# A channel shuffle in 28 tiles in place of 24: most tiles 20 KB a partition instead of 24 KB, five load buffers instead of four

## The chip, the cores and the metric

The kernel runs on 1 core of one Trainium2 chip. The metric is the device time of one execution in microseconds (us). The experiments ran in three batches on three chips, each batch with its own runs of the kernel before, so differences are taken within a batch.

## The reference

The input is 16 x 64 x 64 x 256 float32 (67.1 MB). In each row of 256 channels, 8 groups of 32 channels are transposed to 32 groups of 8. Nothing is computed.

```python
x = x.reshape(batch, h, w, groups, channels_per_group)
x = x.transpose(0, 1, 2, 4, 3)
x = x.reshape(batch, h, w, c)
```

## The kernel before

The array is cut into tiles of 128 partitions. A size `q` of the list below is in rows of 256 floats, so in KB, a partition. Each tile is loaded by one transfer from the SP queue, copied with the shuffle by the Vector engine (DVE), and stored by one transfer from the ACT queue. All buffers of a pool are as large as the largest tile.

```python
_SIZES = [4, 4, 8] + [24] * 20 + [16]
_IN_BUFS = 4
_OUT_BUFS = 4
...
    first = 0
    for q in _SIZES:
        in_tile = in_pool.tile([P, biggest * c], F32, name="in_tile")
        nc.sync.dma_start(out=in_tile[:, : q * c], in_=rows(x_flat, first, q))
        out_tile = out_pool.tile([P, biggest * c], F32, name="out_tile")
        nc.vector.tensor_copy(
            out=out_tile[:, : q * c].rearrange("p (i j g) -> p i j g", j=CPG, g=G),
            in_=in_tile[:, : q * c].rearrange("p (i g j) -> p i j g", g=G, j=CPG),
        )
        nc.scalar.dma_start(out=rows(out_flat, first, q), in_=out_tile[:, : q * c])
        first += P * q
...
```

Of the kernel before, what the change touches and what calls it, by code (L numbers as in the profile page):

```python
# [1 line left out]

# [4 lines left out]


F32 = mybir.dt.float32
P = 128  # L10

_SIZES = [4, 4, 8] + [24] * 20 + [16]
_IN_BUFS = 4
_OUT_BUFS = 4


@with_exitstack
def kernel(
    ctx: ExitStack,
    tc: tile.TileContext,  # L20
    x: bass.AP,
    groups: bass.AP,
    out: bass.AP,
):
    nc = tc.nc
    b, h, w, c = x.shape
    G = int(groups)
    CPG = c // G
    assert G * CPG == c
    assert sum(_SIZES) * P == b * h * w  # L30
    biggest = max(_SIZES)

    x_flat = x.rearrange("b h w c -> (b h w c)")
    out_flat = out.rearrange("b h w c -> (b h w c)")

    in_pool = ctx.enter_context(tc.tile_pool(name="in_pool", bufs=_IN_BUFS))
    out_pool = ctx.enter_context(tc.tile_pool(name="out_pool", bufs=_OUT_BUFS))

    def rows(flat, first, q):

        return flat[first * c : (first + P * q) * c].rearrange("(p f) -> p f", p=P)

    ctx.enter_context(tc.manual_schedule(engines=None))
# [13 lines that stand above are left out]
# [1 line left out]
_INS = ['x', 'groups']  # L58
_OUTS = [((16, 64, 64, 256), 'float32')]

_NUMBERS = {'groups': 8}


# [26 lines left out]
```

## Time and profile before

| kernel before | |
|---|---|
| time | 317.67 us, median of 3 (317.63 to 317.87) |
| profiled span | 315.2 us |
| DVE busy | 122.2 us, 39% |
| two DMA queues together | 99.4% of 16 engines |
| bytes | 134.22 MB, half in, half out |

How to read it: the two DMA shares are of the span of all 16 engines, so their sum says how much bandwidth is left. The lines themselves are in the prediction. Two more views matter later, and the prediction does not show them. The first is the order of instructions around one load's issue. In the order of instructions the columns are start, length (us), engine, line, operation; an SPq row is a load being issued, an ACTq row a store.

```profile
107.54 5.69 DVE L49 COPY out_tile<-in_tile 128x6144 f32<-128x6144 f32 x1 [8.81 <-DMA in_tile<-in_x_dram]
113.26 0.33 SPq L47 DMA_DIRECT2D in_tile<-in_x_dram  x1
113.27 0.36 ACTq L53 DMA_DIRECT2D out_dram<-out_tile  x1
```

The copy ends at 113.23 us, and only then is the next load issued, into the buffer that the copy has emptied. The second is the other half of the load queue's waits. The prediction quotes only its waits for copies (98.0 us); the same answer has a larger line above it, in which the queue waits for an earlier load to land:

```profile
SPq L47 <- DMA in_tile<-in_x_dram: 124.7, 17, 8.4
```

In each turn the queue first waited for that landing and then, 5.8 us more, for the copy.

### The profile page before, as it was taken

What the parts mean: (1) busy time and instruction counts of PE and PEld (TensorE: products, weight loads), DVE (VectorE), ACT (ScalarE), POOL (GpSimd) and SP (SyncE); (2) the same over time, 40 slices, a digit from 0 to 9 for tenths busy, and PEclk for the clock granted to TensorE, in tenths of its full rate; (3) what the DMA queues carried; (4) which work ended last, traced back from release to release, by engine and by line L of the source; (5) the groups of instructions that cost most, each with busy time, mean ns of one, the idle gap of its engine ahead of it and who ended that gap; (6) DMA issues with size and microseconds to landing.
All of it is one profiled execution on the core that took longest, in us unless ns stands there. A gap on an engine that the chain in (4) does not pass through costs nothing.

```text
span 315.2 us, 178 instructions
## 1 busy us (share of the span) xinstructions
DVE 122.2 (39%) x24; POOL 0.2 (0%) x4
## 2 busy tenths in 40 slices
DVE  2277517070625335260707162442517070625400
POOL 0000000000000000000000000000000000000000
DMA  8999999999999999999999999999999999999997
GB/s 316 399 458 407 423 424 446 430 421 446 437 415 446 437 418 443 440 415 443 440 415 443 443 412 443 446 409 443 446 415 437 446 415 437 443 420 431 431 437 319
DMA packets 6912, 134.22 MB, mean 426 GB/s; under 512 B 768, under 2 KB 768, under 8 KB 1280
## 3 DMA queue, kind: packets, MB, share of 16 engines
q1 hardware_dynamic: 3456, 67.11, 49.9%
q10 hardware_dynamic: 3456, 67.11, 49.5%
HBM read 67.11 MB, written 67.11 MB: 426 GB/s over the span
## 4 chain that ended last, share of the span: by engine, by line
DMA 38%; another core or an unknown queue 30%; DVE 25%; issue 0%; DVEq 0%
DMA in_tile<-in_x_dram 38%; DVE out_tile L49 25%; DVEq L49 0%
## 5 line engine op out<-in xcount | busy, mean ns | idle before, releaser
L49 DVE COPY out_tile<-in_tile 128x6144 f32<-128x6144 f32 (+3 forms) x24 | 122.2, 5093 | 175.9 <-DMA in_tile<-in_x_dram 175.7
L71 POOL MEMSET const-bfloat16-1.0<- 128x1 bf16 x1 | 0.1, 101 | 0.0
L71 POOL MEMSET const-uint8-127<- 128x1 uint8 x1 | 0.1, 101 | 0.0
L71 POOL MEMSET const-float32-0.0<- 128x1 f32 x1 | 0.1, 98 | 0.2 <-issue 0.2
L71 POOL MEMSET const-float32-1.0<- 128x1 f32 x1 | 0.1, 98 | 0.0
## 6 DMA issues: line engine op xcount, KB each, us to landing
in_tile<-in_x_dram SPq DMA_DIRECT2D x20, 3072.0 KB, 52.3
out_dram<-out_tile ACTq DMA_DIRECT2D x20, 3072.0 KB, 40.1
in_tile<-in_x_dram SPq DMA_DIRECT2D x1, 2048.0 KB, 49.9
out_dram<-out_tile ACTq DMA_DIRECT2D x1, 2048.0 KB, 16.3
in_tile<-in_x_dram SPq DMA_DIRECT2D x2, 512.0 KB, 3.8
in_tile<-in_x_dram SPq DMA_DIRECT2D x1, 1024.0 KB, 6.2
out_dram<-out_tile ACTq DMA_DIRECT2D x2, 512.0 KB, 16.8
out_dram<-out_tile ACTq DMA_DIRECT2D x1, 1024.0 KB, 27.1
```

The lines of the kernel that those rows point to most:

```text
L49: nc.vector.tensor_copy(out=out_tile[:, : q * c].rearrange("p (i j g) -> p i j g", j=CPG, g=G), in_=in_tile[:, : q * c].rearrange("p (i g ...
L71: nc = _bacc.Bacc("TRN2", target_bir_lowering=False, num_devices=1)
```

## The change

The intent: smaller tiles in the steady part, and one more load buffer for the space that they free (5 x 20 + 4 x 20 = 180 KB a partition, before 4 x 24 + 4 x 24 = 192).

```diff
-_SIZES = [4, 4, 8] + [24] * 20 + [16]
-_IN_BUFS = 4
+_SIZES = [4, 4, 8] + [20] * 24 + [16]
+_IN_BUFS = 5
 _OUT_BUFS = 4
```

## The prediction

> **What bounds the kernel now.** I read the page first, then stretches of the span, then the order of instructions, then the waits. The page:
>
> ```profile
> span 315.2 us, 178 instructions
> DVE 122.2 (39%) x24; POOL 0.2 (0%) x4
> DVE  2277517070625335260707162442517070625400
> DMA  8999999999999999999999999999999999999997
> DMA packets 6912, 134.22 MB, mean 426 GB/s; under 512 B 768, under 2 KB 768, under 8 KB 1280
> q1 hardware_dynamic: 3456, 67.11, 49.9%
> q10 hardware_dynamic: 3456, 67.11, 49.5%
> ```
>
> DVE is idle 61% of the time; the DMA row is full from the second slice to the last but one, and the two queues (q1 loads, q10 stores) together fill 99.4% of what 16 engines could give. So the time is the bytes plus whatever the engines lose at the two ends. The stretches (length, then DVE busy and copies, POOL, clock, DMA share, GB/s) show where they lose:
>
> ```profile
> 0.00:4.00 4.00, 0.00 (x0) 0.20 (x4) 1.00 0.57 200
> 4.00:36.00 32.00, 16.62 (x6) 0.00 (x0) 1.00 1.02 426
> 36.00:281.00 245.00, 96.05 (x17) 0.00 (x0) 1.00 1.00 432
> 294.00:308.50 14.50, 3.86 (x1) 0.00 (x0) 1.00 1.00 432
> 308.50:315.20 6.70, 0.00 (x0) 0.00 (x0) 1.00 0.73 313
> ```
>
> Only the first 4 us (nothing moves for 1.7 us) and the last 6.7 us are not full. Counting packets in flight in the trace's own packet records gives the same: never fewer than 16 (one per engine) between 16 us and 308 us, and under 0.03 us of idle engine time between 4 and 16 us.
>
> The trap is the other view. The groups by form and the waits say that DVE waits for loads, and the load queue for copies:
>
> ```profile
> L49 DVE COPY out_tile<-in_tile 128x6144 f32<-128x6144 f32 x20 | 114.2, 5708 | 163.7 <-DMA in_tile<-in_x_dram 163.7
> L49 DVE COPY out_tile<-in_tile 128x4096 f32<-128x4096 f32 x1 | 3.9, 3861 | 6.5 <-DMA in_tile<-in_x_dram 6.5
> SPq L47 <- DVE out_tile L49: 98.0, 19, 5.9
> in_tile<-in_x_dram SPq DMA_DIRECT2D x20, 3072.0 KB, 52.3
> out_dram<-out_tile ACTq DMA_DIRECT2D x20, 3072.0 KB, 40.1
> ```
>
> It looks as if a fifth load buffer would remove 163.7 us of idleness. But a load takes 52.3 us from issue to landing while one tile period is 14.54 us (copies of 24 KB start at 49.38 and, 16 periods later, at 282.07: 232.69/16). So 52.3/14.54 = 3.6 loads are always standing in the queue, and 40.1/14.54 = 2.8 stores. Neither queue is ever empty; DVE waits for bandwidth, not for a buffer.
>
> The end is drained the same way:
>
> ```profile
> 282.07 5.71 DVE L49 COPY out_tile<-in_tile 128x6144 f32<-128x6144 f32 x1 [8.87 <-DMA in_tile<-in_x_dram]
> 294.24 3.86 DVE L49 COPY out_tile<-in_tile 128x4096 f32<-128x4096 f32 x1 [6.47 <-DMA in_tile<-in_x_dram]
> ```
>
> The last copy is over at 298.1 us, but the packet records show the first row of its store leaving at 308.5 us: two 24 KB stores stand before it. The last copy has 10 us to spare.
>
> **What the Trainium skill says.** (1) "DMA: Bandwidth & Descriptors", section Bandwidth, gives a fabric ceiling of 435.2 GB/s for the 16 engines; the trace's 432 is 99% of it. The same section says that for transfers between HBM and SBUF the per-core HBM share (~358) binds; this trace, with one core running, does not agree. (2) The same page, "Queues, rings and completion order": each engine goes round between the queues it has work for, packet by packet. The trace agrees: the first store's 8 rows of 4 KB per engine would need 8 x 159 ns = 1.3 us alone, but by the packet records they went from 9.29 to 17.20 us, taking turns row by row with a load's rows of 24 KB. (3) "Perfetto Trace Analysis", DMA Optimizations: larger transfers are better, with overhead above all under 2 KB. All data rows here are 4 KB or more; the packets under 2 KB are the 768 four-byte semaphore writes (16 for each of 48 transfers). (4) "VectorE: DVE Perf Modes", section on the TRN2 errata: a copy has a fixed cost of about 150 cycles. The trace: (5708 - 3861)/2048 = 0.902 ns an element, leaving 3861 - 4096 x 0.902 = 166 ns fixed, which fits.
>
> **The change part by part.** Bytes: none added (4 + 4 + 8 + 24 x 20 + 16 = 512 rows of 1 KB a partition, as before). Transfers: 28 loads and 28 stores in place of 24 and 24.
>
> Packets: the packet records have one length for each row size in the undisturbed stretch: 159 ns for 4 KB, 309 for 8, 611 for 16, 912 for 24. That is a straight line: (912 - 159)/20480 B = 0.03677 ns per byte, and 8 ns fixed; a 20 KB row should read 761 ns. In one period an engine moves 8 load rows, 8 store rows and two semaphore writes. The bytes cost 16 x 24576 x 0.03677 = 14,458 ns of the 14,543 ns period, so 85 ns a load-store pair are fixed (packets overlap a little, so this is less than 16 x 8 + 2 x 9). With 20 KB: 16 x 20480 x 0.03677 + 85 = 12,048 + 85 = 12,133 ns. Twenty-four of these are 291.19 us; twenty of the old are 290.86 us. **Sum: +0.33 us**, equally four more pairs at 85 ns. All of it is on the path, since the engines are the path.
>
> Copies: a 20 KB copy is 5120 x 0.902 + 166 = 4784 ns; 24 of them 114.8 us against 114.2, so DVE goes to about 122.8 us busy. Beside a 12.13 us period that is hidden. Issues: eight more, 0.33 to 0.36 us each in the record, on two queues that run several tiles ahead. Hidden.
>
> Load buffers, 4 to 5: five times 20 KB hold 100 KB a partition against 96, so look-ahead in bytes hardly moves. What it does move is the latency: load i+5 is issued when copy i ends and lands five periods after load i, so issue to landing = 5 x 12.13 - 4.8 - 0.1 = 55.8 us. (Check on before: 4 x 14.54 - 5.7 - 0.1 = 52.3, as measured.) It becomes 4.6 loads standing in place of 3.6. Worth nothing, since the queue was never empty.
>
> Store buffers stay at four, but hold 80 KB in place of 96. Before, store plus copy took 40.1 + 5.7 = 45.8 us of the 58.2 us that four periods give, 12.4 us spare. After, the first stores (4, 4, 8 KB) still pair off row by row with three large loads, so stores stay three tiles behind loads: 3 x 12.13 + 2.2 (the offset before: 45.8 - 3 x 14.54) = 38.6 us of 48.5, about 10 us spare, and 33.8 us from issue to landing. No new wait.
>
> Ends: the first three tiles and the last are the same, so first byte at 1.7 us and the last store's 16 KB rows are too. Over 294 us the drain has two 20 KB stores before the last one, so the last copy still has about 8 us to spare. Gain 0.
>
> **The rivals.** *A, the fifth buffer keeps the load queue fuller.* For it: the 163.7 us of DVE idleness and the load queue's 98.0 us of waiting for copies. Against: the full DMA row. Even if it removed every fixed nanosecond between tiles it could give 20 x 0.085 = 1.7 us: 316.0 us. *B, smaller tiles fill and drain the pipeline faster*, about a sixth of one 24 KB copy and store at each end: 1 us of copy or 1.2 us of store, 316.5 us. Against: both ends run at full DMA rate with the copy's 10 us to spare, and the closing tile is the same 16 KB. *C, each transfer has an exposed completion*, some 0.5 us by this trace (last row of the fourth load over at 16.09 us, its copy starts at 16.63 us): eight more would be +4 us, 322 us. Against: the next transfer's rows follow while that completion travels, and the period leaves only 85 ns a pair. *D, the row pitch of 20 KB meets the memory badly* (or 24 KB did). Against: rows of 4, 8, 16 and 24 KB are on one line, so the limit is per byte and not in the address pattern. A 1% change of rate would be 3 us either way. *E, four smaller store buffers make copies wait.* Against: the 10 us spare. If wrong, DVE would wait for stores, but loads already queued would keep the engines busy for a while; +1 us.
>
> **Range and chances.** 317.67 + 0.33 = 318.0 us. The three runs of before spread by 0.24 us, and different phases of the engines at the end (their last rows end up to 0.7 us apart) could move it by half a microsecond. B pulls a little down, C and D a little up: 317.3 to 318.8. For 2% it would have to leave 311.3 to 324.0; the lower edge asks for a rate above the one that all row sizes show, the upper one for a defect in C, D or E several times larger than I see. Faster 0.005, same 0.98, slower 0.015.
>
> **What would show it right or wrong.** Right: a period of 12.13 us between 20 KB copies of 4.78 us, DMA share 1.00 at about 432 GB/s in the middle, 8064 packets (before 6912), load landing 55.8 us and store landing about 34 us, DVE still waiting for loads only, by about 7.3 us. Wrong: a DMA row with a hole in the middle (A or E; E also shows DVE waiting for stores), a period that is off 12.13 at a full DMA share (C or D; D shows 20 KB packets away from 761 ns), or a last copy that ends less than a few microseconds before its store's first row leaves (B).

## The result, and the profile after

318.35 us, median of 6 (318.00 to 318.64), against 317.72 us, median of 6, for the kernel before in the same rounds. The ratio is 1.0022, with a 95% interval of 1.0009 to 1.0035. The ratios here are from the fast runs of the same rounds; they differ slightly from the ratio of the medians. Executions over 1.5% slower than the fastest of the same kernel are left out of the means. The difference is small but clear of noise, and the time is inside the predicted range.

The page of the changed kernel:

```profile
span 316.4 us, 201 instructions
DVE 122.9 (39%) x28; POOL 0.2 (0%) x4
DMA  8999999999999999999999999999999999999996
DMA packets 8064, 134.22 MB, mean 424 GB/s; under 512 B 896, under 2 KB 896, under 8 KB 1408
q1 hardware_dynamic: 4032, 67.11, 49.8%
q10 hardware_dynamic: 4032, 67.11, 49.4%
```

The same picture: a DMA row without a hole, DVE at 39%. Stretches of it (start:end, length, DVE busy and copies, POOL, clock, DMA share, GB/s):

```profile
4.00:36.00 32.00, 17.21 (x6) 0.00 (x0) 1.00 1.01 421
36.00:281.00 245.00, 97.05 (x21) 0.00 (x0) 1.00 1.00 432
308.50:316.40 7.90, 0.00 (x0) 0.00 (x0) 1.00 0.68 289
```

The middle moves 432 GB/s as before. Groups by form, and the issues with their median time to landing:

```profile
L49 DVE COPY out_tile<-in_tile 128x5120 f32<-128x5120 f32 x24 | 114.8, 4784 | 166.3 <-DMA in_tile<-in_x_dram 166.3
in_tile<-in_x_dram SPq DMA_DIRECT2D x24, 2560.0 KB, 48.5
out_dram<-out_tile ACTq DMA_DIRECT2D x24, 2560.0 KB, 32.4
```

The copy takes 4784 ns, to the nanosecond what the prediction worked out. A store lands 32.4 us after its issue (forecast 33.8). A load lands 48.5 us after its issue, which is not the 55.8 us that the prediction forecast. The order of instructions shows why:

```profile
105.47 12.47 SPq L47 DMA_DIRECT2D in_tile<-in_x_dram  x2
105.53 4.80 DVE L49 COPY out_tile<-in_tile 128x5120 f32<-128x5120 f32 x1 [7.38 <-DMA in_tile<-in_x_dram]
110.36 12.46 ACTq L53 DMA_DIRECT2D out_dram<-out_tile  x2
```

(The first and last rows merge two issues each; their starts are what matters.) The load is now issued at 105.47 us, just before the copy starts, and not at 110.33 us, when the copy ends. It waits for the landing of an earlier load, not for a buffer. The waits of the load queue say the same; the line for copies is gone:

```profile
SPq L47 <- DMA in_tile<-in_x_dram: 227.8, 21, 11.9
```

The semaphores behind those waits (a semaphore is the counter by which a transfer reports that it has landed): in both kernels all transfers report on the same eight semaphores (99 to 101 and 103 to 107 in the trace), in the steady part taken in turn, loads and stores alternating. A ninth transfer waits until the one eight places earlier has landed. For a load that is the load four tiles before: in the changed kernel a steady load is issued 0.06 us after that landing, in the kernel before 5.8 us after it. So in the steady part at most four loads are in flight, even with five or eight buffers, and issue to landing should be 4 x 12.13 = 48.5 us. It is. A queue that simply holds no more than four loads is ruled out by the start: there the changed kernel has five in flight, on five different semaphores. The eight semaphores belong to the program as it was built; no run changed their number.

### The profile page after: what moved, and what is told of

Same layout as the page of the kernel before. It is cut to its first block, busy times and chain, and to the rows that moved or that the text cites. A ratio compares the mean times of both kernels' runs of the same rounds, so it can differ in the third digit from the quotient of the medians.

```text
span 316.4 us, 201 instructions
## 1 busy us (share of the span) xinstructions
DVE 122.9 (39%) x28; POOL 0.2 (0%) x4
## 2 busy tenths in 40 slices
DMA packets 8064, 134.22 MB, mean 424 GB/s; under 512 B 896, under 2 KB 896, under 8 KB 1408
## 4 chain that ended last, share of the span: by engine, by line
DMA 93%; DVE 2%; issue 0%; SPq 0%; DVEq 0%
DMA in_tile<-in_x_dram 90%; DMA out_dram<-out_tile 4%; DVE out_tile L49 2%; SPq L47 0%; DVEq L49 0%
## 5 line engine op out<-in xcount | busy, mean ns | idle before, releaser
L49 DVE COPY out_tile<-in_tile 128x5120 f32<-128x5120 f32 (+3 forms) x28 | 122.9, 4388 | 179.4 <-DMA in_tile<-in_x_dram 179.3
## 6 DMA issues: line engine op xcount, KB each, us to landing
in_tile<-in_x_dram SPq DMA_DIRECT2D x24, 2560.0 KB, 48.5
out_dram<-out_tile ACTq DMA_DIRECT2D x24, 2560.0 KB, 32.4
```

What stands on the lines that cost most here:

```text
L49: nc.vector.tensor_copy(out=out_tile[:, : q * c].rearrange("p (i j g) -> p i j g", j=CPG, g=G), in_=in_tile[:, : q * c].rearrange("p (i g ...
```

## The experiments

"Pair" is one load and one store. The theories: **P**, each added pair costs a fixed 85 ns of engine time, and nothing else of the change costs. **L**, eight completion semaphores limit loads in flight to four. **N**, a pair costs twice as much. **S**, five loads at the start open a hole there. **C**, from the prediction, each transfer has an exposed completion. **A**, look-ahead in buffers is worth time. **E**, copies that wait for stores cost time. Differences are of the means of the fast runs in the same rounds. "Buffers" are load and store buffers. The first four rows are the first batch, the next four the second, the last four the third. All kernels gave correct results.

| run | tiles | buffers | pairs to before | median us | ratio (95%) | mean difference us |
|---|---|---|---|---|---|---|
| after_again | 20 KB | 5/4 | +4 | 318.46 | 1.0030 (1.0017 to 1.0043) | +0.90 |
| e1_20k_4_4 | 20 KB | 4/4 | +4 | 318.49 | 1.0026 (1.0012 to 1.0040) | +0.84 |
| e2_24k_5_3 | 24 KB | 5/3 | 0 | 317.91 | 1.0003 (0.9989 to 1.0017) | +0.12 |
| e3_8k_5_4 | 8 KB | 5/4 | +40 | 321.75 | 1.0128 (1.0113 to 1.0142) | +4.08 |
| before_again | 24 KB | 4/4 | 0 | 317.73 | 0.9996 (0.9984 to 1.0009) | -0.14 |
| e4_12k_8_4 | 12 KB | 8/4 | +20 | 319.63 | 1.0065 (1.0053 to 1.0078) | +2.05 |
| e5_32k_3_3 | 32 KB | 3/3 | -5 | 317.40 | 0.9988 (0.9974 to 1.0001) | -0.40 |
| e6_20k_2_4 | 20 KB | 2/4 | +4 | 319.51 | 1.0058 (1.0045 to 1.0070) | +1.81 |
| e7_32k_even | 32 KB, no small ones | 3/3 | -8 | 324.59 | 1.0203 (1.0178 to 1.0227) | +6.79 |
| e8_16_32k | 16, 15 x 32, 16 | 3/3 | -7 | 316.93 | 0.9982 (0.9968 to 0.9995) | -0.63 |
| e9_20k_1_4 | 20 KB | 1/4 | +4 | 520.47 | single run | |
| e10_20k_5_2 | 20 KB | 5/2 | +4 | 318.81 | 1.0043 (1.0029 to 1.0058) | +1.32 |

### The changed kernel again, and the size without the fifth buffer

> The changed kernel once more, to see how much of its +0.63 us is steady. Theory P (85 ns of fixed engine time for each added load-store pair, 4 pairs): +0.33 us on before, period 12.13 us. Rival N (the pairs cost about twice that, 170 ns each, as the first comparison suggests): +0.7 us. Rival S (five loads issued at the start delay the third load and open a hole of some 0.2 us in the first 8 us): the third load lands at about 9.1 us again and idle engine time between 4 and 8 us is about 0.2 us again (before 0.03).

```diff
 _SIZES = [4, 4, 8] + [20] * 24 + [16]
-_IN_BUFS = 5
+_IN_BUFS = 4
```

> The size alone: 20 KB tiles with four load buffers. Theory L (the completion semaphores go round among eight transfers, so a load waits for the load four before it and a fifth buffer is never used): period 12.13 us, load from issue to landing 4 x 12.13 - 4.8 - 0.1 = 43.6 us, time within 0.3 us of the changed kernel. Rival A (the fifth buffer is worth something): slower than the changed kernel by over 1 us. Rival S: the third load lands at about 7.9 us as before, and the time is some 0.2 us below the changed kernel.

Again +0.90 us, and +0.84 us with four buffers: the fifth buffer is worth nothing, and rival A falls. The changed kernel's loads landed after 48.5 us again; those of the kernel with four buffers:

```profile
in_tile<-in_x_dram SPq DMA_DIRECT2D x24, 2560.0 KB, 43.6
```

With four buffers a load waits for the copy again (43.6 us, as theory L forecast); with five it is issued a copy's length earlier and stands that much longer in a queue that was not empty. The idle engine time between 4 and 8 us was 0.24 us in the first profile of the changed kernel, 0.15 in the second and 0.07 with four buffers; the third load landed as late with four buffers as with five. Rival S gains no footing: the time did not fall with the hole.

### The fifth buffer at the old size

```diff
 _SIZES = [4, 4, 8] + [24] * 20 + [16]
-_IN_BUFS = 4
-_OUT_BUFS = 4
+_IN_BUFS = 5
+_OUT_BUFS = 3
```

> The fifth load buffer alone, at the old size (one store buffer less, or it doesn't fit). Theory L: load from issue to landing 4 x 14.54 = 58.2 us; the prediction's own account (a load is issued when the copy five before it ends): 5 x 14.54 - 5.7 - 0.1 = 66.9 us. Three store buffers give 43.6 us a turn where store and copy took 45.8 us, so copies should wait about 2 us for stores, but DMA stays full: 317.7 us within 0.4. Rival E (copies that wait for stores cost time): 1 us or more slower than before. Rival S: five loads at the start, so 0.2 us slower than before and the third load late.

No difference in time. In the issues and the waits:

```profile
in_tile<-in_x_dram SPq DMA_DIRECT2D x20, 3072.0 KB, 58.1
```

```profile
DVE out_tile L49 <- DMA out_dram<-out_tile: 171.5, 21, 9.0
```

58.1 us is 4 x 14.54: theory L, and not the 66.9 us of the prediction's own account. The second line is worth a pause: DVE now waits 171.5 us for stores instead of loads, and the time is the same. What DVE, which is not the bound here, waits for says nothing about the time of this run; I had expected some 2 us of such waiting a tile, but the whole idle time went over to the other releaser. Rival E finds nothing here.

### Many more pairs

```diff
-_SIZES = [4, 4, 8] + [20] * 24 + [16]
+_SIZES = [4, 4, 8] + [8] * 60 + [16]
```

> Sixty tiles of 8 KB in place of twenty of 24 KB: 40 more load-store pairs than before, ten times the lever of the change. Theory P: 40 x 0.085 = +3.4 us, period 16 x 8192 x 0.03677 + 85 = 4904 ns, 321.1 us. Rival N (170 ns a pair): +6.9 us, 324.6 us. Rival C (an exposed completion of 0.5 us for each transfer): +40 us. Load from issue to landing by theory L 4 x 4.9 = 19.6 us, by the buffers 5 x 4.9 - 2.0 - 0.1 = 22.4 us.

```diff
-_SIZES = [4, 4, 8] + [20] * 24 + [16]
-_IN_BUFS = 5
+_SIZES = [4, 4, 8] + [12] * 40 + [16]
+_IN_BUFS = 8
```

> Forty tiles of 12 KB with eight load buffers: 20 more pairs than before. Theory P (85 ns a pair): +1.7 us on before, 319.3 us, or up to +2.2 if every size but 24 KB carries the further 0.4 us seen so far. Theory L (a load waits for the load four before it): period 16 x 12288 x 0.03677 + 85 = 7.31 us, load from issue to landing 4 x 7.31 = 29.2 us, although there are eight buffers; by the buffers alone it would be 8 x 7.31 - 2.9 - 0.1 = 55.5 us.

Two copies of the 8 KB kernel, 35 tiles apart (their order in time), give its period, and below them the issues of the 12 KB kernel:

```profile
85.57 2.05 DVE L49 COPY out_tile<-in_tile 128x2048 f32<-128x2048 f32 x1 [2.86 <-DMA in_tile<-in_x_dram]
...
257.29 2.02 DVE L49 COPY out_tile<-in_tile 128x2048 f32<-128x2048 f32 x1 [2.86 <-DMA in_tile<-in_x_dram]
```

```profile
in_tile<-in_x_dram SPq DMA_DIRECT2D x40, 1536.0 KB, 29.2
```

(257.29 - 85.57)/35 = 4.906 us; forecast 4.904. So the 85 ns per pair in the steady part hold over a threefold range of sizes, and no larger charge per transfer is hidden: N and an exposed completion (C) fall. The whole time rises by 4.08 us for 40 pairs and 2.05 us for 20, so about 0.10 us a pair where the steady part alone would give 3.4 and 1.7. The 2.05 us hold an accident: three of the five executions took 319.55 to 319.63 us (+1.77 us on average, 88 ns a pair) and two took 320.22 and 320.38. The first of these two was profiled, and it lost 0.8 us in two steps of 7.73 us between copies (215.85 to 231.32 us), where the steps around them average 7.31, as forecast. No view shows why. And eight load buffers still give 29.2 us = 4 x 7.3, not 55.5: theory L once more.

### The kernel before again

> The kernel before once more, for a second profile: its first one fell on a run of 317.02 us, where most of its runs are at 317.6 to 317.9. Theory T (the first profile of before was one of its few quick executions; its ends lost 3.6 us where those of all later profiles lost 4.3 to 4.8 us, counted as last packet less what the packets need): this profile loses 4.2 to 4.6 us and its engines finish up to 1.3 us apart. Rival Z (24 KB tiles with four load buffers lose less at the ends than all the others): 3.6 us again.

Its profile fell on a quick execution again (317.05 us; its others took 317.68 to 318.10). Packet records: its 16 engines end their last rows between 313.41 and 314.12 us, a spread of 0.71 us; in the first profile of before 0.72; in the changed kernel 1.41 and 1.23; in the 24 KB run with five buffers, whose profiled execution was an ordinary one (317.96 us), 1.51. So the expectation of a slower profile missed, and theory T and rival Z were not told apart by it: an ordinary 24 KB run does show the wide spread, but with other buffers.

### Fewer pairs

```diff
-_SIZES = [4, 4, 8] + [20] * 24 + [16]
-_IN_BUFS = 5
-_OUT_BUFS = 4
+_SIZES = [4, 4, 8] + [32] * 15 + [16]
+_IN_BUFS = 3
+_OUT_BUFS = 3
```

> Fifteen tiles of 32 KB with three load and three store buffers (192 KB, as before): 5 pairs fewer. Theory P: 5 x 0.085 = -0.43 us, 317.2 us; period 16 x 32768 x 0.03677 + 85 = 19.36 us, copies about 7.6 us, load from issue to landing 3 x 19.36 - 7.6 - 0.1 = 50.4 us. Rival (every size but 24 KB carries a further 0.4 us): 317.6 us, no gain. Rival A (three buffers are too few): over 319 us with holes in the DMA row.

-0.40 us, forecast -0.43, although the interval just reaches 1. Three buffers are enough.

```diff
-_SIZES = [4, 4, 8] + [20] * 24 + [16]
+_SIZES = [32] * 16        # e7;  e8: [16] + [32] * 15 + [16];  both with 3 and 3 buffers
```

> Sixteen equal tiles of 32 KB, three load and three store buffers, no small tiles at the ends: 8 pairs fewer than before. Theory P (85 ns a pair, ends hidden): 317.67 - 0.68 = 317.0 us. Rival B (the small first and last tiles are needed to fill and drain): the first copy can only start when 4 MB have landed (about 12 us) and the last store waits for a 7.5 us copy; if the stores then standing are too few, the DMA row has a hole near the end and the time is 319 us or more.

> 16 KB, fifteen tiles of 32 KB, 16 KB, three and three buffers: 7 pairs fewer than before, with a short last copy (3.9 us). Theory P: 317.67 - 0.60 = 317.1 us and no hole in the DMA row; if the even one shows rival B's hole at the end, this one should not.

e8 is the version that the pairs point to: 316.93 us, -0.63 us against before (forecast -0.60), the lowest median: 0.2% below before, which is clear of noise. Against the changed kernel it was not run in the same rounds. e7, with one pair less, is 6.8 us slower. Stretches of e7 and, below, of e8:

```profile
36.00:281.00 245.00, 89.87 (x12) 0.00 (x0) 1.00 1.00 425
294.00:308.50 14.50, 5.48 (x1) 0.00 (x0) 1.00 0.90 389
308.50:324.30 15.80, 1.97 (x1) 0.00 (x0) 1.00 0.65 278
```

```profile
36.00:281.00 245.00, 95.89 (x13) 0.00 (x0) 1.00 1.01 434
294.00:308.50 14.50, 3.85 (x1) 0.00 (x0) 1.00 1.00 431
```

Two things, then. The hole that rival B foresaw is there: share 0.90 and 0.65 at the end, because the last copy ran from 303.0 to 310.5 us and too few stores stood before it (the packet records show 5.3 us of idle engine time after 294 us). And the middle is slower at a full share, 425 for 434 GB/s: a tenth of the load rows (204 of 2048) took over 1347 ns where most took 1213. I did not foresee that. Why e7 has such rows all through the run and e8, with rows of equal size, only 25 of 1920, all between 14 and 18 us, stays open. It may also mean that the prediction's rival D, an address or ordering pattern that slows some rows, is not empty in general, although no 20 KB or 24 KB run showed it.

### How few buffers are enough

```diff
 _SIZES = [4, 4, 8] + [20] * 24 + [16]
-_IN_BUFS = 5
+_IN_BUFS = 2              # e6;  e9: 1
```

> 20 KB tiles with two load buffers in place of five. If the load queue only has to be non-empty: steady period still 12.13 us, load from issue to landing 2 x 12.13 - 4.8 - 0.1 = 19.4 us (1.6 loads standing), and a loss only at the start, where the third load cannot be issued until the first copy ends at 5.2 us: +1 to +2 us on the changed kernel, 319.5 to 320.5. Rival A (look-ahead in buffers is what carries this kernel): the period grows and the time is over 325 us.

> 20 KB tiles with a single load buffer, so that load and copy alternate: here the buffers must bind. A load and the store of the tile before start together and share the engines for 12.1 us, then some 2 us of completion and start-up and the 4.8 us copy pass with no load in flight: period 18 to 19 us, 24 of them 430 to 455 us, DMA share in the middle about 0.65.

e6, stretches:

```profile
4.00:6.00 2.00, 1.82 (x2) 0.00 (x0) 1.00 0.30 119
6.00:8.00 2.00, 0.38 (x1) 0.00 (x0) 1.00 0.92 152
36.00:281.00 245.00, 95.92 (x20) 0.00 (x0) 1.00 1.00 432
```

Two load buffers run the middle at the full 432 GB/s and lose only at the start, where the queue is empty at 4 to 6 us: 319.51 us, as forecast. With one buffer the queue is empty once in every tile (e9, stretches):

```profile
205.00:210.00 5.00, 0.00 (x0) 0.00 (x0) 1.00 0.87 373
210.00:215.00 5.00, 4.75 (x1) 0.00 (x0) 1.00 0.00 0
215.00:220.00 5.00, 0.04 (x1) 0.00 (x0) 1.00 0.78 262
```

While the copy runs (210.25 to 215.04 us) nothing moves. The mean share in the middle is 0.67 (expected 0.65), but the period is 19.9 us, more than the 18 to 19 us expected. The packet records of this turn divide it: 4.8 us of copy, 1.0 us from its end to the load's first row (216.03 us), 12.9 us for the load's rows (to 228.98 us), 1.2 us from there to the next copy (230.14 us). So start and completion expose 2.2 us, as expected; what was too low is the 12.1 us for the rows. The store's first row leaves 1.7 us after the load's, and some of the load's rows take well over 761 ns (20 of 128 over 800 ns); how much each adds was not separated. That is what "buffers bind" looks like, and neither kernel of the change is near it.

```diff
 _IN_BUFS = 5
-_OUT_BUFS = 4
+_OUT_BUFS = 2
```

> 20 KB tiles with five load buffers and two store buffers. If only an empty queue costs: DVE waits for stores in place of loads (a store and its copy get 2 x 12.13 = 24.3 us a turn), DMA share stays 1.00, period 12.13 us, time as the changed kernel, 318.4 us within 0.3. Rival E (copies that wait for stores cost time): 2 us or more slower. All 20 KB kernels so far took 1.92 us outside the profiled span, all others 1.78: this one should show 1.92 if it is the program and not chance, the two 32 KB ones 1.78.

318.81 us, 0.4 to 0.5 us above the changed kernel (which ran in other rounds), so neither of the two expected values. The time outside the profiled span, expected at 1.92 us, was 2.05. DVE waits for stores, as in e2, and the middle is full; but at the end, where with two store buffers no more than one store can stand beside a copy, a stretch loses a tenth:

```profile
36.00:281.00 245.00, 97.38 (x21) 0.00 (x0) 1.00 1.01 432
294.00:304.00 10.00, 4.80 (x1) 0.00 (x0) 1.00 0.91 392
```

Rival E seems right there in a small way: copies that wait for stores cost nothing while loads are left to fill the engines, and something once there are none.

## Why the prediction was right, and where not

**Right.** Both kernels are held by the 16 DMA engines; 134.22 MB at 432 GB/s set the time. The middle kept share 1.00 and 432 GB/s. The changed kernel's copies started at 69.13 and, 14 tiles later, at 238.96 us: a period of 12.131 us, forecast 12.133. The 20 KB rows took 761 ns, 8064 packets moved, DVE was busy 122.9 us, and the last copy ended at 302.3 us while the packet records show its store's first row at 308.9 us, so there was 6.6 us to spare (estimated 8). The range held all six runs, but thanks to the half microsecond that it allowed for the ends: the sum itself gave 318.0 us, and no run of the changed kernel was below that.

**The step on look-ahead failed.** The prediction said that load i+5 is issued when copy i ends and so needs 55.8 us. It needs 48.5 us, because eight completion semaphores in turn allow four loads in flight; e2 (58.1), e3 (19.6) and e4 (29.2) all give four periods. The step was checked on the kernel before, where the buffer wait happened to be the later of the two, and so the check could not show the other limit. The line of 124.7 us was the hint, though not a proof: a buffer, too, is free only after its load has landed. It changed no time, since the queue was never empty. The fifth buffer is thus doubly useless: in the steady part it cannot be used, and it is not needed.

**The sum was small by half.** Forecast +0.33 us; measured +0.71, +0.90 and, without the fifth buffer, +0.84 in the same rounds. Over all 40 executions of before (mean 317.66 us) and all 17 of the two 20 KB kernels with four or five load buffers (318.41), it is +0.74 us. Of this, 0.33 us are the four pairs, shown by the period at three sizes (8 KB 4.906 us, 20 KB 12.131, and 19.36 for the 32 KB tiles of e8, whose copies start at 73.46 and, 11 tiles later, at 286.42 us; forecast 19.36) and supported by the times of e5 and e8 in the other direction. 0.14 us lie outside the profiled span: the execution takes 1.92 us longer than its span in 20 KB kernels (five profiles), 1.77 or 1.78 us in those of 8, 12, 24 and 32 KB (eight profiles), and 2.05 us in e10; no view shows what happens there. The remaining 0.27 us must be at the ends, since nothing else is left: in the profiles, first and last engine end 1.2 to 1.5 us apart in the 20 KB kernels with four or five load buffers and four store buffers, and 0.7 us in the two of before, both of which fell on quick executions. Whether that is the size or the draw of the execution is not settled; e2 speaks for the draw, the longer time of e3 (about 0.7 us above 85 ns a pair) for the size. e4 speaks for neither: without its two longer executions it is within 0.1 us of 85 ns a pair.

**Rivals.** A is refuted (e1, e4; e6 loses only at the start). B is refuted for the change, but e7 shows that its mechanism is real when the last tiles are large and the stores standing are few. C is refuted (e3, where it would have cost 40 us). D did not occur at 20 or 24 KB, and something that may be of its kind did in e7. E cost nothing in e2 and, as far as runs of different rounds can be compared, half a microsecond in e10.

**A reading of the skill that was too narrow.** The prediction's point (1) took one sentence on 358 GB/s for what the section says of a core that runs alone; the first point of the list at the end puts it right. No sum rests on it.

## What to carry to other kernels

When the transfer engines are full, ask of a buffer only whether the queue ever runs empty: two load buffers filled these engines in the steady part as well as five (they lost 1 us at the start), and one did not. Before a buffer is added, look at what the issue waits for, since a limit on transfers in flight can make it unusable. Then what is left is the count of transfers (here 0.08 to 0.10 us a load-store pair, all in, at 8, 12 and 32 KB; at 20 KB 0.19, of which the pairs explain less than half) and the two ends, where the last tile should be small enough for its copy to end while stores are still standing (16 KB in e8, against 32 KB in e7).

## What the Trainium skill lacked or had wrong

- "DMA: Bandwidth & Descriptors", section Bandwidth, has one sentence that misleads when it is read alone, as the prediction read it: that for transfers between HBM and SBUF the per-core share of about 358 GB/s binds. Its own table, taken on one core with the pair's other core idle, reaches 425 GB/s. With one core running, reads and writes together held 432 GB/s here for 245 us; no run here had a second core at work.
- The same page, section "Queues, rings and completion order", has an engine drain a packet of typically 9 to 17 descriptors before it turns to another queue. Here each row is one packet in the records, and where a store of 4 KB rows met a load of 24 KB rows, the two queues took turns row by row: the store's eight rows per engine took 7.9 us, for an estimated 1.3 us alone (8 x 159 ns).
- No page read here tells that a program whose transfers take eight completion semaphores in turn holds no more than four loads in flight; a fifth to eighth load buffer then goes unused in the steady part (landing 4 periods after issue: 48.5, 58.1, 29.2, 19.6 us).
- "DMA: Bandwidth & Descriptors", in its anatomy of a transfer, gives about 2.0 us of fixed cost, measured on the software-descriptor path; these transfers are issued from the SP and ACT queues, for which it has no such sum. When load and copy alternate (one buffer), 2.2 us a turn were exposed. When the queue stays filled, a load-store pair costs only 85 ns.
- "VectorE: DVE Perf Modes", in its tier table, has a float32 copy of 2048 elements at 1227 ns. This copy, which reads with a stride of 32 elements, took 2006 to 2042 ns in the kernels that have that size. The table says nothing of strided reads; "SBUF — State Buffer", in its note on cachelines, tells of a penalty for accesses that leave a 16-byte line, but not how large it is for this engine. No run here copies without the stride, so that the stride is the reason is not shown.
